# A hybrid decoder block on one core: first projection ahead of its norm, recurrence woven with attention, output projection in halves, first keys computed ahead of the ranking

## The chip, the cores and the metric

The kernel runs as one program on one core of a Trainium2 chip. The metric is the device time of that program in microseconds (us), as the median of the runs shown. TensorE is PE here (PEld is its weight loads), VectorE is DVE, ScalarE is ACT, GpSimd is POOL, SyncE is SP, whose queue issues nearly all transfers.

## The reference, cut to what matters

512 tokens of width 1024 go through one block:

```
h = rms_norm(x) ; p = h @ w_in                     # 2464 columns used, in 20 tiles of 128
rwkv columns: p + mu * (p[token - 1] - p), then a recurrence over tokens, 8 heads of 64
attention columns: + bias, window of 128 tokens, softmax with a sink, 8 query and 2 key heads
x = x + [y_rwkv, rms_norm(y_attn)] @ w_out
h2 = rms_norm(x)
per head (8), per half (2):  scores of 128 keys = (h2 @ wq) @ subkeys ; top 16 of each
best 16 of the 256 pairs -> softmax gates ; expert rows u, v ; y = sum gate * gelu(h2 . u) * v
out = rms_norm(x + y)
```

## The kernel before, in words

All float32 products of wide operands are made as three passes over operands split into a high part and a remainder (`split`, L163 to L166: a cast on ACT, then a subtraction on DVE or POOL; `mm3_`, L172 to L178: 8 chunks of 128 rows, three matmuls each, so 24 matmuls of 512 columns for one tile).

**Front.** `x` arrives transposed in eight pieces (L92). The first norm (`rms`, L208) sums squares over the chunks, takes the root on DVE (`rsqrt`) and broadcasts it over the partitions through PE; then each chunk of `x` is scaled by weight and root (L248) and split. `proj` makes one tile of columns; `shifted` (L286) mixes a tile with its previous token: two copies on ACT out of PSUM (L291, L293) and one combination on DVE (L294). `prepare(j)` makes the operands of head pair j, `products(j)` the triangular solves and products inside chunks of 64 tokens (L406 is the products `pg`, in tiles of 64 by 64 of the array). `weave` interleaves, in program order, the steps of `prepare(j+1)` and `products(j)`; for the last j, `attention_columns` stands for `prepare`. Then comes `recurrence()`, a chain over 8 chunks of 64 tokens (L614 to L646) with `group_norm` of each 128 tokens, and after it in program order `attention()`: 8 parts, each with scores (L676), mask (L678), maximum (L683), exponentials (L691), division by the sum on DVE (L698), transposes (L714), output (L720), and `out_norm` of each 128 tokens. Outside the blocks marked `manual_schedule`, a planner orders each engine's instructions when the kernel is built: what stands earlier in the program goes first among what it reckons ready, so later work fills gaps. PSUM tiles of the front come from four tags of two banks each (`proj`, `chain`, `tinv`, `att`); recurrence and `group_norm` use `chain` and `proj`.

**Turn to the retrieval.** The residual `x2T` is loaded (L815) when its SBUF, shared with the recurrence's tiles, comes free. The output projection makes 8 tiles of 512 tokens (L822 adds), each adding its square to the second norm's sum; then root, broadcast, 32 transposes of `x` to rows (L850), scaling by the norm (L858) and splits, three of eight remainders on DVE and five on POOL.

**Ranking.** A loop over 16 halves of heads (hc), in the order written out by hand on every engine: the key product `pq` (24 matmuls of 512), copy, scores `psc` (L1047), copy, and `top` on DVE (five kinds of instruction on four tiles, L929 to L937); between them `steps(ups, n)` puts in half products of the dense operand `pA` (12 matmuls of 384), and `choose` ranks pairs. Weights are loaded and split one to three hc ahead.

**Dense.** One-hots and gates are built on DVE while `pA` goes on; then 128 blocks of gated `v` are accumulated (L1269 to L1271). None of this is in the diff.

Of the kernel before, what the change touches and what calls it, by code (L numbers as in the profile page):

```python
# [13 lines left out]
OP = mybir.AluOpType  # L14
# [61 lines left out]
def _emit(ctx, tc, A, out, dbg, stop):  # L76
# [5 lines left out]
    keep = ctx.enter_context(tc.tile_pool(name="keep", bufs=1))  # L82
# [5 lines left out]

    xst, xp = right("xp")
# [6 lines left out]
    SY.dma_start(sink, A["sink"])  # L96
# [146 lines left out]
    rb = xp.tile([128, S], F32, name="rb")  # L243
    SC.copy(rb, pb)
    hhi, hlo = hl("h")
    for k in range(KD):
        h = xp.tile([128, S], F32, name="h", tag="h", bufs=3)
        V.scalar_tensor_tensor(h, xT[:, k, :], vcol(C_LN1 + k), rb, op0=OP.mult, op1=OP.mult)  # L248
        split(hhi[:, k, :], hlo[:, k, :], h)
    xst.close()  # L250
# [16 lines left out]
    def load_w(src, name="w"):  # L267
        his, los = [], []
        for hf in range(2):
            ks = slice(4 * hf, 4 * hf + 4)  # L270
            w = wst.tile([128, 4, 128], F32, name=name, tag="w", bufs=3)
            SY.dma_start(w, src[:, ks])
            whi = wst.tile([128, 4, 128], F32R, name=name + "h", tag="wh", bufs=4)
            wlo = wst.tile([128, 4, 128], F32R, name=name + "l", tag="wl", bufs=4)
            split(whi, wlo, w)
            his += [whi[:, k] for k in range(4)]
            los += [wlo[:, k] for k in range(4)]
        return his, los

    def proj(i, m=128):  # L280
        whi, wlo = load_w(A["w_in"][i])
        p = pt("proj", "pj")
        yield from mm3_(p[:m], whi, wlo, hhi, hlo, m=m)
        return p[:m]

    def shifted(i, dst, pool, m=128):  # L286

        p = yield from proj(i, m)
# [10 lines left out]
    pst, prep = right("prep")  # L299

# [8 lines left out]
    def lora():  # L309
        yield from shifted(0, la, prep)  # L310
# [81 lines left out]
    def products(j):  # L392
# [4 lines left out]
        for x in range(2):  # L397

            for ch in range(2):
                pg = pt("tinv", "pg", (128, 4, 128))  # L400
                for c in range(4):
                    ts = slice((4 * ch + c) * 64, (4 * ch + c) * 64 + 64)
# [4 lines left out]
                    if c == 1:  # L407
                        yield
                for p in range(2):
                    orow = slice(64 * p, 64 * p + 64)  # L410
                    for g_, cl in ((gA, slice(0, 64)), (gR, slice(64, 128))):
                        V.tensor_tensor(out=g_[orow, 4 * ch:4 * ch + 4, p ^ x, :], in0=pg[orow, :, cl],
                                        in1=gmask[orow, None, cl].to_broadcast([64, 4, 64]), op=OP.mult)
                yield
# [10 lines left out]
        BK = rwk.tile([128, 8, 2, 64], F32, name=f"BK{j}")  # L425
        for ch in range(2):
            pk = pt("tinv", "pk", (128, 4, 2, 64))
            for c in range(4):
                ts = slice((4 * ch + c) * 64, (4 * ch + c) * 64 + 64)
# [329 lines left out]
    for _ in recurrence():  # L759
        pass  # L760
# [638 lines left out]
```

## Time and profile before

| what | value |
|---|---|
| time, median of 3 runs | 1654.14 us (1652.88 to 1655.71) |
| the profiled execution's own time | 1651.63 us |
| its span | 1649.9 us |
| PE, PEld busy in the span | 96%, 83% |
| DVE, ACT, POOL busy | 78%, 40%, 43% |
| granted clock of PE, mean | 0.992 |

The shares are means over stages with different limits, and a matmul's modelled end reaches past the start of the next one, so a busy PE is not a full PE: its pace is read from starts. Times of rows count from the start of the span.

### The profile page before, as it was taken

To read this page: it belongs to the slowest core of one execution; us is meant where nothing else is said; L and a number is where in the kernel's file an instruction comes from. 1 tells how busy PE (TensorE), PEld (TensorE's weight loads), DVE (VectorE), ACT (ScalarE), POOL (GpSimd) and SP (SyncE) were. 2 spreads that over 40 slices of the span, in tenths; PEclk is the share of its full clock that TensorE was granted. 3 is DMA by queue.
4 is the path that set the end of the run, shared out by engine and by line. 5 is a ranking of instruction groups with operands and counts; after the bars stand their busy time and mean duration, and the time that the engine had idled before them with its cause. 6 is when DMAs were issued, how large, how long until landed. Compare 5 with 4: busy or idle time off the path is not lost.

```text
span 1649.9 us, 30181 instructions
## 1 busy us (share of the span) xinstructions
PE 1584.4 (96%) x11629; PEld 1362.9 (83%) x11629; DVE 1279.5 (78%) x2474; ACT 655.2 (40%) x1078; POOL 712.3 (43%) x670
## 2 busy tenths in 40 slices
PE   5999999898999989999999999999999999999997
PEld 4777677676898889888888888888888888888886
DVE  5656548745799989999868778877878877787797
ACT  5444345534343435445433333333333333333334
POOL 5112110033577612222235555555565655556582
PEclk9999999999999999999999999999999999999999
DMA  4111120141222249998999988988988989889794
GB/s 135 53 41 41 53 60 2 58 166 52 90 103 91 78 162 318 331 360 316 337 325 354 330 308 298 332 311 304 341 304 310 319 310 325 306 289 352 244 305 147
DMA packets 180113, 369.57 MB, mean 224 GB/s; under 512 B 17792, under 2 KB 102272, under 8 KB 179712
## 3 DMA queue, kind: packets, MB, share of 16 engines
q1 hardware_dynamic: 137056, 225.14, 40.0%
q0 software_dynamic: 36864, 134.23, 22.4%
q10 hardware_dynamic: 6048, 8.26, 1.4%
q8 instruction: 91, 1.49, 0.4%
q14 instruction: 54, 0.44, 0.1%
HBM read 332.04 MB, written 35.52 MB: 223 GB/s over the span
## 4 chain that ended last, share of the span: by engine, by line
PE 49%; DVE 11%; DMA 3%; issue 2%; ACT 1%; SPq 0%; POOL 0%; DVEq 0%; POOLq 0%; ACTq 0%
PE acc L1271 10%; PE acc L1269 10%; PE acc L1270 10%; PE pA L177 7%; PE pA L175 7%; PE pA L176 7%; DVE O L1140 3%; DVE ul L166 2%; DVE scr L1094 2%; DVE P L1145 2%; DMA u<-in_uT_dram 1%; DMA row<-in_vB_dram,ix 0%; DMA gts<-gates 0%; DMA acts<-actd 0%; PE pG L1167 0%
## 5 line engine op out<-in xcount | busy, mean ns | idle before, releaser
L177 PE MATMUL pA<-h2hi,ul 128*128 128x384 f32 x1024 | 348.3, 340 | 10.2 <-DVE ul L166 6.1
L175 PE MATMUL pA<-h2hi,uh 128*128 128x384 f32 x1024 | 354.0, 346 | 3.0 <-ACT uh L165 1.6
L176 PE MATMUL pA<-h2lo,uh 128*128 128x384 f32 x1024 | 346.4, 338 | 0.0
L1271 PE MATMUL acc<-vl,wh 128*128 128x512 f32 x768 | 299.1, 389 | 1.1 <-DVE vl L166 1.1
L1269 PE MATMUL acc<-vh,wh 128*128 128x512 f32 x768 | 299.5, 390 | 0.6 <-ACT vh L165 0.6
L1270 PE MATMUL acc<-vh,wl 128*128 128x512 f32 x768 | 299.3, 390 | 0.0
L1081 POOL DMA_INDIRECT row<-in_u_dram,ix x128 | 175.6, 1372 | 284.8 <-DVE scr L1094 246.5
L1081 POOL DMA_INDIRECT row<-in_vB_dram,ix x128 | 195.9, 1530 | 142.5 <-DVE x L1092 118.9
L166 DVE TENSOR_TENSOR vl<-v,vh 128x1024 fp32r<-128x1024 f32 x128 | 217.1, 1697 | 35.9 <-ACT vh L165 35.0
L177 PEld LDWEIGHTS pA<-h2hi,ul 128*128 128x128 f32 x1024 | 193.3, 189 | 15.3 <-DVE ul L166 11.2
L175 PEld LDWEIGHTS pA<-h2hi,uh 128*128 128x128 f32 x1024 | 193.4, 189 | 6.8 <-ACT uh L165 2.1
L176 PEld LDWEIGHTS pA<-h2lo,uh 128*128 128x128 f32 x1024 | 193.4, 189 | 3.0
L1092 DVE SCALAR_TENSOR_TENSOR x<-row,ac,x 128x1024 f32<-128x1024 f32 x128 | 172.6, 1348 | 6.0 <-DMA row<-in_vB_dram,ix 4.2
L1271 PEld LDWEIGHTS acc<-vl,wh 128*128 128x128 f32 x768 | 144.2, 188 | 32.6 <-DVE vl L166 2.1
L1269 PEld LDWEIGHTS acc<-vh,wh 128*128 128x128 f32 x768 | 144.2, 188 | 28.5 <-ACT vh L165 0.9
L1270 PEld LDWEIGHTS acc<-vh,wl 128*128 128x128 f32 x768 | 144.1, 188 | 27.4
L1094 DVE SCALAR_TENSOR_TENSOR scr<-row,h2g 128x1024 f32<-128x1024 f32 x128 | 158.8, 1240 | 1.5 <-DMA row<-in_u_dram,ix 0.2
L165 ACT CAST uh<-u 128x1024 fp32r<-128x1024 f32 x128 | 133.9, 1047 | 61.3 <-PE pA L176 33.0
L166 DVE TENSOR_TENSOR ul<-u,uh 128x1024 fp32r<-128x1024 f32 x109 | 134.8, 1238 | 21.2 <-ACT uh L165 20.9
L165 ACT CAST vh<-v 128x1024 fp32r<-128x1024 f32 x128 | 134.0, 1047 | 0.1
L1168 ACT ACTIVATE gst<-pG 128x512 f32<-128x512 f32 x96 | 55.9, 597 | 100.6 <-PE pG L1167 98.8
L888 ACT ACTIVATE act<-pA 128x384 f32<-128x384 f32 x86 | 42.2, 491 | 132.6 <-PE pA L177 132.6
(711 smaller groups left out, 2508.0 us busy)
## 6 DMA issues: line engine op xcount, KB each, us to landing
u<-in_uT_dram SPq DMA_DIRECT2D x128, 512.0 KB, 8.1
v<-in_vB_dram SPq DMA_DIRECT2D x128, 512.0 KB, 6.3
gts<-gates SPq DMA_DIRECT2D x384, 64.0 KB, 5.1
gates<-gst SPq DMA_DIRECT2D x11, 2048.0 KB, 11.8
w<-in_w_in_dram SPq DMA_DIRECT2D x40, 256.0 KB, 3.2
wq<-in_wq_dram SPq DMA_DIRECT2D x16, 512.0 KB, 3.5
acts<-actd ACTq DMA_DIRECT2D x42, 192.0 KB, 6.1
act<-acts SPq DMA_DIRECT2D x42, 192.0 KB
```

The lines of the kernel that those rows point to most:

```text
L165: (hi_eng or SC.copy)(dst_hi, src)
L166: (lo_eng or V).tensor_tensor(out=dst_lo, in0=src, in1=dst_hi.bitcast(F32), op=OP.subtract)
L175: mm(ps, whi[k][:, :m], ahi[:, k], start=k == 0, stop=False)
L176: mm(ps, whi[k][:, :m], alo[:, k], start=False, stop=False)
L177: mm(ps, wlo[k][:, :m], ahi[:, k], start=False, stop=k == KD - 1)
L1081: GP.indirect_dma_start(r_, None, A["vB"].rearrange("b p d -> (b p) d") if w_ else A["u"], bass.IndirectOffsetOnAxis(ap=ix[:, w_, jj:jj + ...
L1092: V.scalar_tensor_tensor(x2[:, 0, :], r_, ac[:, jj:jj + 1], x2[:, 0, :], op0=OP.mult, op1=OP.add)
L1094: V.scalar_tensor_tensor(scr, r_, 1.0, h2g, op0=OP.mult, op1=OP.mult, accum_out=ac[:, jj:jj + 1])
L1168: SC.activation(gst[:, :, :, t4 * 4:t4 * 4 + 4].rearrange("p n g t -> p (n g) t"), p.rearrange("p t e -> p e t"), AF.Copy, scale=1.0 / GS)
L1269: mm(o, wh[:, ts], vh[:, ds_], start=b == 0, stop=False)
L1270: mm(o, wl[:, ts], vh[:, ds_], start=False, stop=False)
L1271: mm(o, wh[:, ts], vl[:, ds_], start=False, stop=b == 127)
```

## The change

The first projection (column tile 0) is made from `x` times the norm's weight alone, ahead of the norm; the norm's factor `rb` is multiplied into every projected tile on DVE as it leaves PSUM, and ACT's copy goes. `products` issues its 64-by-64 products for both operands side by side. Attention keeps one key tile and takes 64 of its rows for each key head; its division moves to POOL. Recurrence and attention are woven. The output projection goes over tokens 0 to 255 first (tiles 5, 6, 7, 0 to 4), then over 256 to 511; the norm, transposes and key products of the first half stand among the second half's tiles, and key products 0 and 1 are done before the ranking. Key weights 2 and 3 and the first block of `u` are loaded and split earlier; `ln2r` is loaded later.

```diff
-    for k in range(KD):
-        SY.dma_start(xT[:, k, :], A["xT"][:, k, :])
     vec = consts.tile([128, NVEC], F32, name="vec")
     SY.dma_start(vec, A["vec"])
+    for k in range(2):
+        SY.dma_start(xT[:, k, :], A["xT"][:, k, :])
...
+    first[0] = load_w(A["w_in"][0])
+    for k in range(2, KD):
+        SY.dma_start(xT[:, k, :], A["xT"][:, k, :])
     take, scale, spread = rms(xp, KD, D, "n1", V)
-    for k in range(KD):
-        take(k, xT[:, k, :])
-    scale()
-    pb = spread()
...
-        V.scalar_tensor_tensor(h, xT[:, k, :], vcol(C_LN1 + k), rb, op0=OP.mult, op1=OP.mult)
+        V.tensor_scalar(h, xT[:, k, :], vcol(C_LN1 + k), None, op0=OP.mult)
         split(hhi[:, k, :], hlo[:, k, :], h)
+        take(k, xT[:, k, :])
+    with tc.manual_schedule(engines={mybir.EngineType.PE}):
+        p0 = proj(0)
...
+        scale()
+        pb = spread()
+    rb = prep.tile([128, S], F32, name="rb", tag="rb")
+    SC.copy(rb, pb)
...
-        SC.copy(pr[:m, 1:S + 1], p)
-        pm = pool.tile([128, S], F32, name="pm", tag="pm", bufs=1)
-        SC.activation(pm[:m], p, AF.Identity, scale=omu[:m, i:i + 1])
-        V.scalar_tensor_tensor(dst, pr[:m, 0:S], vec[:m, C_MU + i:C_MU + i + 1], pm[:m],
+        V.tensor_tensor(out=pr[:m, 1:S + 1], in0=p, in1=rb[:m], op=OP.mult)
+        SC.activation(dst, pr[:m, 1:S + 1], AF.Identity, scale=omu[:m, i:i + 1])
+        V.scalar_tensor_tensor(dst, pr[:m, 0:S], vec[:m, C_MU + i:C_MU + i + 1], dst,
...
+            pg = [pt("tinv", "pg", (128, 4, 128)) for x in range(2)]
+            for c in range(4):
+                for x in range(2):
                     for p in range(2):
-                        mm(pg[orow, c, :], (k if x else B)[rows, ts], AR[rows, 4 * ch + c, :], start=True, stop=True)
+                        mm(pg[x][orow, c, :], (k if x else B)[rows, ts], AR[rows, 4 * ch + c, :], start=True, stop=True)
...
-            SC.activation(q, p, AF.Identity, bias=vcol(C_BATT + j))
+            V.tensor_tensor(out=q, in0=p, in1=rb, op=OP.mult)
+            SC.activation(q, q, AF.Identity, bias=vcol(C_BATT + j))
...
-        weave(prepare(j + 1) if j < 3 else attention_columns(), WS[j], products(j), 23)
+        weave(prepare(j + 1) if j < 3 else attention_columns(), WS[j], products(j), 15)
...
-                mm(pS[kv][:, e, w0:], qT[2 * jj + e][:, tk], kP[kv][:, ks], start=True, stop=True)
+                rows = slice(64 * kv, 64 * kv + 64)
+                mm(pS[kv][:, e, w0:], qT[2 * jj + e][rows, tk], kP[rows, ks], start=True, stop=True)
...
-                V.tensor_scalar(Ps[:, kv, e, w0:], Ps[:, kv, e, w0:], sm[:, kv, e:e + 1], None, op0=OP.mult)
+                GP.tensor_scalar(Ps[:, kv, e, w0:], Ps[:, kv, e, w0:], sm[:, kv, e:e + 1], None, op0=OP.mult)
...
-    for _ in recurrence():
-        pass
-    for _ in attention():
-        pass
+    weave(recurrence(), 35, attention(), 64)
...
-            if hc < 2:
+            if hc < 4:
                 wqs[hc] = pool_u.tile([128, KD, 128], F32, name="wq", tag="u", bufs=4)
...
-    for i in range(KD):
-        whi, wlo = load_w(A["w_out"][i])
...
+    def out_weights(i):
+        if i < 2 or i > 4:
+            wo[i] = load_w(A["w_out"][i])
+            return
...
+    def out_tile(i, h):
+        whi, wlo = wo[i]
+        p = pt(("proj", "chain")[i % 2], "pj")[:, 0:256]
+        for _ in mm3_(p, whi, wlo, yhi[:, :, HS[h]], ylo[:, :, HS[h]]):
+            pass
+        V.tensor_tensor(out=xT[:, i, HS[h]], in0=xT[:, i, HS[h]], in1=p, op=OP.add)
+        square(i, h)
...
+    for i in (5, 6, 7, 0, 1, 2, 3, 4):
+        out_weights(i)
+        out_tile(i, 0)
     pe_ = ExitStack()
     pe_.enter_context(tc.manual_schedule(engines={mybir.EngineType.PE}))
+    out_tile(0, 1)
+    norm_sums(0)
+    wq_load(0)
+    wq_load(1)
+    out_tile(1, 1)
+    out_tile(2, 1)
+    pb = norm_spread(0)
...
+    for i in range(3, KD):
+        for k in range(2 * (i - 3), min(KD, 2 * (i - 2))):
+            rows(k, 0)
+            normed(k, 0, pb)
+        if i > 4:
+            out_weights(i)
+        out_tile(i, 1)
...
+    key_product(0, 0)
+    norm_sums(1)
+    key_product(1, 0)
+    pb = norm_spread(1)
     for k in range(KD):
+        normed(k, 1, pb)
+    for k in range(KD):
+        rows(k, 1)
+        if k == 3:
+            key_product(0, 1)
+    key_product(1, 1)
...
-        up_split(0)
         for n, b in enumerate(B):
...
-    wq_load(2)
+    up_split(0)
+    wq_split(2)
     for hc in range(16):
...
-        if hc:
+        if hc > 1:
             wq_split(hc + 1)
-        wq_load(hc + 3)
-        whi, wlo = wqs.pop(hc)
...
+        if hc:
+            wq_load(hc + 3)
+        if hc < 2:
+            q = q01[:, hc]
+        else:
+            whi, wlo = wqs.pop(hc)
...
+        if hc == 2:
+            ln2r = mp.tile([128, D], F32, name="ln2r", tag="lnr")
+            SY.dma_start(ln2r, A["ln2r"])
```

`normed(k, h)` scales and splits 256 tokens of chunk k, with the remainder on POOL where k is no multiple of 3; `rows(k, h)` makes two transposes; `norm_sums` and `norm_spread` are the norm's sum and broadcast for two tiles of 128 tokens; `square` adds squares, nearly all on POOL; `key_product(hc, h)` is `mm3_` over 256 columns with a copy into `q01`.

## Rows read from the trace of the kernel before

**Rows 1.** The busy time of each engine by stage: stretch, its length, then busy us (and instructions) of PE, PEld, DVE, ACT and POOL, the granted clock of PE, the transfers' share and GB/s.
```profile
51.00:237.00 186.00, 184.04 (x3587) 135.18 (x3586) 100.83 (x226) 74.75 (x138) 32.79 (x70) 1.00 0.16 49
237.00:296.00 59.00, 58.06 (x824) 43.94 (x823) 48.48 (x172) 32.86 (x106) 0.00 (x0) 1.00 0.04 11
296.00:335.00 39.00, 34.39 (x225) 25.25 (x225) 29.38 (x114) 20.19 (x53) 1.72 (x2) 0.96 0.19 68
335.00:371.00 36.00, 35.07 (x151) 27.93 (x149) 16.36 (x17) 11.75 (x19) 13.96 (x8) 1.00 0.51 183
391.00:428.00 37.00, 33.01 (x162) 27.29 (x163) 20.63 (x130) 12.22 (x17) 12.59 (x6) 1.00 0.28 100
428.00:546.00 118.00, 118.00 (x619) 105.89 (x618) 111.37 (x599) 45.38 (x62) 83.94 (x65) 1.00 0.26 90
840.00:1649.00 809.00, 799.31 (x3872) 706.92 (x3870) 644.13 (x646) 290.05 (x409) 462.12 (x339) 1.00 0.87 306
```

**Rows 2.** The timeline of the start: start, us, engine, line, operation, out<-in, shapes, count, and in brackets the idle time before it with what ended it.
```profile
3.68 0.63 ACT L215 ACTIVATE n1acc<-xT 128x512 f32<-128x512 f32 x1 [1.59 <-DMA xT<-in_xT_dram]
...
10.50 1.47 DVE L219 TENSOR_TENSOR n1acc<-n1acc,n1sq 128x512 f32<-128x512 f32 x2
...
20.06 0.59 ACT L244 COPY rb<-n1b 128x512 f32<-128x512 f32 x1 [1.85 <-PE n1b L231]
...
22.13 1.22 PE L175 MATMUL pj<-hhi,wh 128*128 128x512 f32 x2 [2.11 <-ACT hhi L165]
...
34.66 0.58 ACT L291 COPY pr<-pj 128x512 f32<-128x512 f32 x1
```

**Rows 3.** The groups of instructions of the first 410 us, shapes kept apart: busy us and mean ns of one, then the idle time before them.
```profile
L291 ACT COPY pr<-pj 128x512 f32<-128x512 f32 x13 | 7.6, 584 | 1.3 <-PE pj L177 0.7 <-DVE TT L479 0.5
L166 DVE TENSOR_TENSOR hlo<-h,hhi 128x512 fp32r<-128x512 f32 x8 | 5.1, 682 | 1.3 <-ACT hhi L165 1.3
L350 DVE TENSOR_TENSOR kk<-kk,pn 128x512 f32<-128x512 f32 x4 | 2.7, 687 | 5.2 <-PE pn L348 5.2
```

**Rows 4.** The timeline of PE alone, at two places of the front and one after the ranking; where a row has a count, its matmuls run up to the start of the next row.
```profile
43.38 1.05 PE L342 MATMUL kss<-hind,ksq 128*128 128x2 f32 x8
44.29 0.48 PE L176 MATMUL pj<-hlo,wh 128*128 128x512 f32 x1
...
60.82 1.96 PE L406 MATMUL pg<-AR,B 64*64 64x128 f32 x32
62.72 0.50 PE L175 MATMUL pj<-hhi,wh 128*128 128x512 f32 x1
...
572.02 0.34 PE L176 MATMUL pA<-h2lo,uh 128*128 128x384 f32 x1
572.20 0.34 PE L177 MATMUL pA<-h2hi,ul 128*128 128x384 f32 x1
```

**Rows 5.** The timeline from the recurrence's first step to the end of attention.
```profile
237.82 0.68 PE L614 MATMUL psa<-SAV,TF 64*64 64x64 f32 x16
...
295.45 0.37 ACT L638 COPY yT<-py 128x256 f32<-128x256 f32 x1 [0.67 <-PE py L636]
...
314.34 0.33 SPq L815 DMA_DIRECT2D x2T<-in_xT_dram  x1
...
316.29 0.68 DVE L166 TENSOR_TENSOR ylo<-yT,yhi 128x512 fp32r<-128x512 f32 x1
...
333.91 0.69 DVE L166 TENSOR_TENSOR ylo<-oT,yhi 128x512 fp32r<-128x512 f32 x1
```

**Rows 6.** The group of attention's division on DVE, in the 98 us from 237 to 335; the columns are those of rows 3.
```profile
L698 DVE TENSOR_SCALAR Ps<-Ps,st 128x256 f32<-128x256 f32 x24 | 7.9, 347 | 0.0
```

**Rows 7.** One instruction of DVE with POOL at work and with POOL idle, and POOL's instruction over it, from the timelines of these engines; then one of POOL's own groups by source line (ns: least, median, most).
```profile
472.06 2.41 POOL L166 TENSOR_TENSOR ul<-u,uh 128x1024 fp32r<-128x1024 f32 x1
473.28 1.27 DVE L993 TENSOR_TENSOR sg__4943<-sg__4943,fi 128x64 f32<-128x64 f32 x1
...
599.27 0.22 DVE L993 TENSOR_TENSOR sg__4943<-sg__4943,fi 128x64 f32<-128x64 f32 x1
...
L460 POOL TENSOR_TENSOR Lb<-LC,lmask x16: 725/740/978, 65.8 to 217.6; 128x256 f32<-128x256 f32 x16
```

**Rows 8.** The timeline from the last output tile to the first scores of the ranking.
```profile
364.51 0.69 DVE L822 TENSOR_TENSOR x2T<-x2T,pj 128x512 f32<-128x512 f32 x1 [4.31 <-PE pj L177]
...
370.11 0.69 DVE L822 TENSOR_TENSOR x2T<-x2T,pj 128x512 f32<-128x512 f32 x1 [4.91 <-PE pj L177]
...
375.86 2.07 PE L231 MATMUL n2b<-ident,n2rs 128*128 128x128 f32 x8 [0.54 <-DVE n2rs L205]
377.72 4.50 PE L850 MATMUL px<-ident,x2T 128*128 128x128 f32 x20
...
382.65 7.17 POOL L166 TENSOR_TENSOR h2lo<-h,h2hi 128x512 fp32r<-128x512 f32 x5 [15.28 <-ACT h2hi L165]
...
391.28 1.16 PE L1047 MATMUL psc<-subk,q 128*128 128x128 f32 x8 [0.68 <-ACT q L1042]
```

**Rows 9.** The timeline of the ranking's second and fifth pass: scores on PE, and the start of `top` on DVE.
```profile
402.76 1.05 PE L1047 MATMUL psc<-subk,q 128*128 128x128 f32 x8
...
428.45 1.05 PE L1047 MATMUL psc<-subk,q 128*128 128x128 f32 x8
430.20 0.87 DVE L929 MAX8 tv<-sc 128x8 f32<-128x128 f32 x4 [5.60 <-ACT sc L1049]
```

More of the change, by code (lines that the diff above doesn't have):

```diff
@@ L519, in attention_columns @@
     def attention_columns():
[L520 to L522 removed]
+        kP = late["kP"] = prep.tile([128, S], F32, name="kP", tag="aup")
         gup = late["gup"] = prep.tile([128, S], F32, name="gup", tag="la")
@@ L832, in _emit @@
-    take(KD - 1, xT[:, KD - 1, :])
-    if stop == "x2":
-        for j in range(KD):
-            SY.dma_start(dbg["y"][:, j, :], yhi[:, j, :].bitcast(F32))
-        SY.dma_start(dbg["x2"], xT)
-        x2st.close()
-        pust.close()
-        mpst.close()
-        front.close()
-        return
+    acc2 = x2p.tile([128, S], F32, name="n2acc")
+    rs2 = consts.tile([128, NT], F32, name="n2rs")
+    wo = {}
+    HS = [slice(0, 256), slice(256, 512)]
+    TS = [(0, 1), (2, 3)]
+    hhi2, hlo2 = None, None
@@ new lines, in out_weights, with square @@
+    def out_weights(i):
+        if i < 2 or i > 4:
+            wo[i] = load_w(A["w_out"][i])
+            return
+        w = x2p.tile([128, KD, 128], F32, name="wo", tag="wo", bufs=2)
+        SY.dma_start(w, A["w_out"][i])
+        whi = x2p.tile([128, KD, 128], F32R, name="woh", tag="woh", bufs=3)
+        wlo = x2p.tile([128, KD, 128], F32R, name="wol", tag="wol", bufs=3)
+        split(whi, wlo, w)
+        wo[i] = [whi[:, k] for k in range(KD)], [wlo[:, k] for k in range(KD)]
+    def square(i, h):
+        cs = HS[h]
+        if i == (5, 0)[h]:
+            SC.activation(acc2[:, cs], xT[:, i, cs], AF.Square)
+            return
+        sq = x2p.tile([128, 256], F32, name="n2sq", tag="n2sq", bufs=2)
+        SC.activation(sq, xT[:, i, cs], AF.Square)
+        (V if i == (4, 7)[h] else GP).tensor_tensor(out=acc2[:, cs], in0=acc2[:, cs], in1=sq, op=OP.add)
@@ new lines, in norm_spread, with rows, normed @@
+    def norm_spread(h):
+        p = pt("att", "n2b", (128, 256))
+        for j, t in enumerate(TS[h]):
+            mm(p[:, j * 128:(j + 1) * 128], rs2[:, t:t + 1].to_broadcast([128, 128]), ident, start=True, stop=True)
+        return p
+    def rows(k, h):
+        p = pt("tinv", "px2", (128, 2, 128))
+        for j, t in enumerate(TS[h]):
+            PE.transpose(p[:, j, :], xT[:, k, t * 128:(t + 1) * 128], ident)
+        SC.copy(x2[:, 2 * h:2 * h + 2, k * 128:(k + 1) * 128], p)
+    def normed(k, h, pb):
+        x = x2p.tile([128, 256], F32, name="h2", tag="h2", bufs=4)
+        V.scalar_tensor_tensor(x, xT[:, k, HS[h]], vcol(C_LN2 + k), pb, op0=OP.mult, op1=OP.mult)
+        split(hhi2[:, k, HS[h]], hlo2[:, k, HS[h]], x, lo_eng=GP if k % 3 else V)
@@ new lines, in key_product @@
+    def key_product(hc, h):
+        whi, wlo = wqs[hc]
+        p = pt(("proj", "chain")[hc], "pq")[:, 0:256]
+        for _ in mm3_(p, [whi[:, k] for k in range(KD)], [wlo[:, k] for k in range(KD)],
+                      hhi2[:, :, HS[h]], hlo2[:, :, HS[h]]):
+            pass
+        SC.copy(q01[:, hc, HS[h]], p)
+    for i in (5, 6, 7, 0, 1, 2, 3, 4):
+        out_weights(i)
+        out_tile(i, 0)
+    hhi2 = h2p.tile([128, KD, S], F32R, name="h2hi")
+    hlo2 = h2p.tile([128, KD, S], F32R, name="h2lo")
@@ L860, in _emit @@
+    norm_sums(1)
+    key_product(1, 0)
+    pb = norm_spread(1)
+    for k in range(KD):
+        normed(k, 1, pb)
[4 more added lines that the diff above has]
+    key_product(1, 1)
+    for hc in range(2):
+        wqs.pop(hc)
+    hhi, hlo = hhi2, hlo2
+    pe_.close()
     front.close()
+    kst.close()
     x2st.close()
@@ L1329, in _emit @@
     pust.close()
+    h2st.close()
     mpst.close()
```

153 lines of the change are left out of this document (71 added, 82 removed).

## The prediction

> **What bounds the kernel now.** I read the busy time by stage first, to see which engine fills which stretch. Up to 237 us PE is nearly full (184.04 of 186 us, modelled) with DVE at half; from 237 to 335 us DVE carries most (48.48 + 29.38 = 77.9 of 98 us), PE has gaps and POOL does 1.7 us; from 335 to 371 PE is full with the output projection; between 391 and 428 DVE works only 20.63 of 37 us; from 428 to 546 PE is full with DVE at 111.37 of 118; behind 840 PE is full to the end [rows 1]. So a time saved ahead of the ranking moves everything behind it forward, and nothing behind it shrinks. Then I read the timeline at the four joints where the front waits: the start, where PE's first projection waits for the norm until 22.13 us [rows 2]; the end of recurrence and attention, where the recurrence's last output is copied at 295.45, its norm ends at 316.97 and attention alone runs on to 334.60 [rows 5]; the second norm, 21.2 us from the last output tile (370.11) to the first scores (391.28) [rows 8]; the first passes of the ranking [rows 9].
>
> **Start (1 us gained, -2 to +4).** Before, the chain is norm, then scaling, then projection. After, PE can start when the first chunk and weights are split, at some 7 us (first chunk landed at 3.68, one small and two weight transfers squeeze in). But DVE now does scaling, remainder and square-add per chunk before PE ends: 8 x 3 x 0.68 = 16.4 us, with two weight remainders of the same size 17.8, so the sum is ready at about 22.5. The norm's own chain, from the last square-add (10.50 + 1.47 = 11.97) to `rb` (20.65), is 8.7 us [rows 2]: `rb` at 31. The first tile left PSUM at 34.66 before; now at 31.5, but the second projection stands behind the norm's matmuls on PE and starts about when it did. One us.
>
> **Products and projections (4 us, -3 to +8).** 19 more evacuations multiply by `rb` on DVE, 0.687 each [rows 3]: 13 us on an engine half free; ACT sheds 13 x 0.584 = 7.6. PE issued 32 of the 64-by-64 products in 1.90 us, 0.059 each [rows 4]; 256 of them are 15.2 us. Side by side in four quarters of the array they take half at best, 7.6 less, and nothing less at worst. The solves' steps are a chain that this doesn't shorten; I take half. The low end is the 13 us of DVE landing partly on waits. Fewer steps in the weave (15 for 23) cost nothing while the count matches the yields.
>
> **Recurrence and attention (12 us, -5 to +20).** The division leaves DVE: 24 x 0.347 = 8.3 us, and eight of half the width, at most 2.8 [rows 6]: 10. DVE's work falls from 77.9 to 68 us. At the share it reached from 237 to 296 (48.48 of 59, 82%) [rows 1] that takes 83 us, and the stage would end at 237.8 + 83 = 321 where it ended at 334.6: 14. The weave gives this by spreading attention so that it has no tail alone behind the recurrence. The score matmuls on 64 rows save PE some time, which is not the bound there: nothing.
> POOL takes 32 divisions. The trace shows none on POOL; between DVE's 0.347 [rows 6] and POOL's two-input product of the same size, 0.740 [rows 7], I take 0.55: 18 us of POOL, which is free, but each part's transposes come 0.8 us later, two parts ahead of need. There is a price: the same DVE addition took 0.22 us with POOL idle and 1.27 with POOL at work [rows 7]. POOL is at work 18 of 83 us, and DVE's two-input instructions meet it for some 2 us in sum: 12 stay. The Trainium skill ("SBUF — State Buffer", on the shared port pair) makes this an exclusive lock: the one that comes second waits for the whole instruction of the other, which the pair of rows agrees with; by it POOL's 18 us could be taken off DVE in the worst case, which is the third case below.
>
> **Output projection to first scores (4 us lost; from 31 lost to 7 gained).** A tile cost 5.60 us (370.11 - 364.51) [rows 8], 0.233 per matmul of 512; one of 384 costs 0.176 [rows 4]; so one of 256 by the same step 0.119. Weights of 128 columns with 2 moving columns came every 0.114 (8 in 0.91 us) [rows 4], so loading them just allows that; the other bound is 0.176, at which the halves would cost 27 us more. At 0.119 a half tile costs 2.86 and halving costs nothing.
> The first half could run beside attention, but its sums need `x2T`, whose transfer was issued at 314.34 when the recurrence's norm released its place [rows 5], and its PSUM tags are the recurrence's. I let two half tiles (5.7 us) be done when the stage ends and 39.1 of the 44.8 us be left, where before 35.5 were left (334.60 to 370.11). Added in between: 16 transposes at 4.50 / 20 = 0.22, 3.6 us, and 1 us of the first half's sums and broadcast. Behind the last half tile: key 0 and key 1 on the first half, 5.7 us, which cover the root; 1.5 of waiting and broadcast; eight chunks scaled and split at POOL's pace, 5 x 7.17 / 10 = 3.6, with the key product ending some 5 us on; transposes 1.8; the last half product 2.9: 17. In sum 60.7 us to the first scores where 56.7 were (334.60 to 391.28): 4 lost. Three weight tiles are loaded and split twice; 1.5 MB and 3 x 2 x 0.68 us of DVE lie under a PE-bound stretch with DVE at 16.36 of 36 [rows 1]; if that cover fails it is 4 us. On SP's queue key weights 2 and 3 wait for slots that keys 0 and 1 free, and the repeated weights stand behind them; that wait ends with a split that needs no output tile.
>
> **First passes of the ranking (8.4 us gained, 5 to 10).** From scores 0 to scores 1 took 402.76 - 391.28 = 11.5 us: the second key product and a wait for the dense operand's split. Now only scores (1.0) and a dense half product, 12 x 0.176 = 2.1, stand there: 3.1. Passes 1 to 4 keep their 25.7 us (to 428.45). DVE follows: it has 16 us idle in that stretch [rows 1], 5.60 of them ahead of the fifth pass [rows 9]. From there on PE's order is the old one. `ln2r` on SP waits only for scores 1: nothing.
>
> **Sum.** 1 + 4 + 12 - 4 + 8.4 = 21.4 us. The profiled execution took 1651.63 us (span 1649.9 and 1.7 around it), 2.5 below the median 1654.14; so 1630.2 by its own time and 1632.7 by the median. I say 1632.
>
> **Rivals.** *The first half is free.* If `x2T` lands before attention ends, six more half tiles (17 us) run in PE's gaps; the gaps would hold some 11. For it: the recurrence is the longer chain's owner of that place and may end early. Against: the weave ends both together. Time 1632 - 11 = 1621.
> *The weave is there already.* Attention filled the recurrence's gaps before, and DVE at 82% may be what the planner gives; with POOL's 18 us taken back from DVE by waits, the stage ends where it did. Time 1632 + 12 = 1644. For it: DVE's rows with POOL at work.
> *Weights bound the halves.* If 256 columns don't come under 0.176, the 20 half products (480 matmuls) cost 480 x 0.057 = 27 us more: 1659, slower. It decides from 0.119 + 21.4 / 480 = 0.164 on. Against: 0.114 for weights alone.
> *Weaving slows the recurrence.* Eight chunks took 57.6 us, 7.2 each; each of three steps may now stand behind an attention instruction on DVE. The other terms give 9.4, so the kernel is slower once the stage ends later than 344; at 12 us a chunk it ends with the norm's 21.5 at 355, 20 late: 1654 - 9.4 + 20 = 1665. Against: the chain's instructions are first whenever they are ready at their turn.
> *Nothing moves*: the stage stays, and the products take DVE's load: within 0.2% of 1654.
>
> **Chances.** The forecast 0.50, the first half free 0.16, the weave there already 0.20, weights 0.04, recurrence slowed 0.05, nothing 0.05. A measurement of this kernel can tell about 0.2% (3.3 us) from no change. Faster is the first three, 0.86; same 0.05; slower 0.09. The range reaches from the second case with its products' high end, 1608, to the third with the products' low end, 1651.
>
> **What would show it.** The first projection's start near 7 us but the first tile out of PSUM near 31; `pg` at 0.03 to 0.06 per matmul; the last remainder of attention near 321, close to the recurrence's norm; matmuls of 256 columns every 0.12 us; `x2T` issued at the end of the recurrence's norm; about 61 us from attention's end to scores 0; scores 1 about 3 us behind scores 0; from the fifth pass on the old pace of PE. Wrong would be: an end of attention past 334, half matmuls above 0.16, or scores 0 to 4 still 37 us apart.

## The result and the profile after

The changed kernel takes 1631.15 us (median of four runs, 1630.73 to 1631.52), the kernel before 1653.51 beside it: a ratio of 0.9865, 95% interval 0.9849 to 0.9882, or 22.4 us. A second set of runs took 1632.52, ratio 0.9875 [0.9859, 0.989]. The forecast was 1632, in a range from 1608 to 1651, so it is 1 us off. The sum is better than its terms, as the stages show: that it comes so near is in part luck. The profiled execution took 1630.73 us, its span 1629.0.

The busy time by stage of the changed kernel, in the columns of [rows 1], cut at its own joints:
```profile
51.00:226.00 175.00, 172.73 (x3561) 128.63 (x3561) 106.54 (x235) 65.64 (x121) 29.87 (x65) 1.00 0.16 50
226.00:293.00 67.00, 64.48 (x863) 47.98 (x861) 53.96 (x173) 38.67 (x130) 26.15 (x31) 1.00 0.02 7
293.00:319.00 26.00, 25.99 (x235) 23.18 (x235) 20.90 (x85) 14.96 (x32) 2.67 (x4) 1.00 0.30 101
319.00:363.00 44.00, 39.08 (x318) 38.91 (x319) 24.29 (x49) 19.29 (x42) 19.74 (x19) 0.96 0.41 151
363.00:380.00 17.00, 15.26 (x114) 13.41 (x113) 8.22 (x26) 8.46 (x22) 5.43 (x36) 1.00 0.35 116
380.00:409.00 29.00, 27.65 (x149) 23.98 (x149) 19.31 (x129) 10.64 (x15) 12.50 (x6) 1.00 0.32 114
409.00:526.00 117.00, 117.00 (x624) 105.95 (x623) 111.90 (x600) 44.65 (x61) 84.52 (x65) 1.00 0.26 91
```
Recurrence and attention (226 to 319) hold 53.96 + 20.90 = 74.9 us of DVE, where [rows 1] have 77.9 before; POOL now does 28.8 us there. From 409 on each engine's load is as before.

The timeline of the start, the answer to [rows 2]:
```profile
9.15 0.79 PE L176 MATMUL pj<-hhi,wh 128*128 128x512 f32 x1 [9.15 <-ACT hhi L166]
...
21.54 0.95 PE L225 MATMUL n1ss<-ones,n1acc 128*128 128x1 f32 x8
...
22.34 0.48 PE L178 MATMUL pj<-hhi,wl 128*128 128x512 f32 x1
...
25.69 1.05 PE L232 MATMUL n1b<-ident,n1rs 128*128 128x128 f32 x8
26.78 0.59 ACT L283 COPY rb<-n1b 128x512 f32<-128x512 f32 x1 [0.79 <-PE n1b L232]
27.40 0.69 DVE L307 TENSOR_TENSOR pr<-pj,rb 128x512 f32<-128x512 f32 x1 [0.69 <-ACT rb L283]
```
The first tile leaves PSUM at 27.40 (34.66 before), and the row at 22.34 belongs to the second projection, which runs while DVE works out the root.

The timeline of recurrence, attention and the first output sums, the answer to [rows 5]:
```profile
225.85 0.68 PE L626 MATMUL psa<-SAV,TF 64*64 64x64 f32 x16
...
292.08 0.37 ACT L650 COPY yT<-py 128x256 f32<-128x256 f32 x1 [0.89 <-PE py L648]
...
313.59 0.33 SPq L826 DMA_DIRECT2D x2T<-in_xT_dram  x1
...
316.80 0.68 DVE L167 TENSOR_TENSOR ylo<-yT,yhi 128x512 fp32r<-128x512 f32 x1
317.49 0.69 DVE L167 TENSOR_TENSOR ylo<-oT,yhi 128x512 fp32r<-128x512 f32 x1
...
322.23 1.41 DVE L860 TENSOR_TENSOR x2T<-x2T,pj 128x256 f32<-128x256 f32 x4 [3.45 <-DMA x2T<-in_xT_dram]
...
322.80 0.55 PE L176 MATMUL pj<-yhi,wh 128*128 128x256 f32 x1 [3.81 <-DVE x2T L860]
```
Both chains now end together (0.69 us apart), and the new wait stands in the last two rows: `x2T`, issued at 313.59 when the recurrence's norm frees its place, is there 8.6 us later, at 322.23, and PE stands still for 3.81.

TensorE alone, at the first scores of the ranking's passes 0, 1 and 4, the answer to [rows 8, 9]:
```profile
380.42 1.06 PE L1132 MATMUL psc<-subk,q 128*128 128x128 f32 x8
383.42 0.83 PE L1132 MATMUL psc<-subk,q 128*128 128x128 f32 x6
...
408.66 1.05 PE L1132 MATMUL psc<-subk,q 128*128 128x128 f32 x8
```

From such rows of every profiled run come the marks below, in us, rounded to 0.1 before they are subtracted: the way from the first `pg` to the first `psa`, from there to the end of the last `ylo` (the stage's end), from there to scores 0, the two together, and scores 0 to scores 4; then the first `pg`, scores 0, and the median of the timed runs. Scores 0 count from their first weight load, at most 0.13 ahead of the matmul's row.
```
                       pg-psa  psa-ylo  ylo-sc0  psa-sc0  sc0-sc4  first pg  sc0     median
before                 177.0    96.8     56.7    153.5     37.0     60.8    391.3   1653.5
changed                172.2    92.4     62.1    154.5     28.2     53.6    380.3   1631.2
changed, again         172.2    92.4     63.0    155.4     28.2     53.1    380.7   1632.5
weave undone           172.6   100.6     55.1    155.7     28.1     54.0    382.3   1633.8
division on DVE        172.2   100.6     62.7    163.3     28.2     52.9    388.4   1638.9
both undone            172.5   110.7     49.9    160.6     28.1     53.8    386.9   1637.9
norm first             174.4    94.2     61.1    155.3     28.2     62.1    391.8   1645.1
products as before     178.9    92.4     60.5    152.9     28.2     53.4    385.2   1640.0
keys 0, 1 late         172.2    92.4     64.1    156.5     35.2     52.8    381.5   1641.4
x2T in 8, SP           172.6    93.9     62.7    156.6     28.2     53.9    383.1   1632.3
x2T in 8, GpSimd       172.5    92.1     57.6    149.7     28.2     53.2    375.4   1629.5
  and weave undone     172.5   108.0     50.7    158.7     28.2     53.4    384.6   1636.8
  and weave 35 to 48   172.2   110.9     50.6    161.5     28.2     53.5    387.2   1635.5
before + weave + div.  177.5    91.5     67.7    159.2     37.1     61.3    398.0   1657.9
```
Where nothing was touched, the way from `pg` to `psa` repeats within 0.4 us and scores 0 to scores 4 within 0.1, but the first `pg` itself only within 1.2, and the way from `psa` to scores 0 differs by 0.9 between the two profiles of the changed kernel. Behind the ranking, from `pG` (the first products of the dense stage) to the end, these two differ by 3 us (1047.3 and 1050.3), so for a single part the marks say more than the total. Each row of marks is one execution; those of "weave undone", "x2T in 8, SP", "weave 35 to 48" and the last row are 3 to 5 us longer than the median of their kernel.

### The profile page after: what moved, and what is told of

The parts are those of the page before. It is cut to its first block, busy times and chain, and to the rows that moved or that the text cites. A ratio compares the mean times of both kernels' runs of the same rounds, so it can differ in the third digit from the quotient of the medians.

```text
span 1629.0 us, 30768 instructions
## 1 busy us (share of the span) xinstructions
PE 1572.6 (97%) x11869; PEld 1366.7 (84%) x11869; DVE 1286.1 (79%) x2497; ACT 652.5 (40%) x1092; POOL 742.4 (46%) x711
## 4 chain that ended last, share of the span: by engine, by line
PE 50%; DVE 11%; DMA 3%; issue 1%; ACT 1%; POOL 1%; SPq 0%; DVEq 0%; ACTq 0%
PE acc L1359 10%; PE acc L1358 10%; PE acc L1357 10%; PE pA L178 7%; PE pA L176 7%; PE pA L177 7%; DVE O L1228 3%; DVE ul L167 2%; DVE scr L1182 2%; DVE P L1233 2%; DMA u<-in_uT_dram 2%; DMA row<-in_vB_dram,ix 1%; DMA v<-in_vB_dram 0%; PE pG L1255 0%; POOL row L1169 0%
## 5 line engine op out<-in xcount | busy, mean ns | idle before, releaser
L176 PE MATMUL pA<-h2hi,uh 128*128 128x384 f32 x1024 | 350.3, 342 | 1.5 <-ACT actd L969 1.5
L1169 POOL DMA_INDIRECT row<-in_u_dram,ix x128 | 175.2, 1369 | 285.7 <-DVE scr L1182 247.7
L167 DVE TENSOR_TENSOR vl<-v,vh 128x1024 fp32r<-128x1024 f32 x128 | 213.9, 1672 | 35.2 <-ACT vh L166 34.4
L178 PEld LDWEIGHTS pA<-h2hi,ul 128*128 128x128 f32 x1024 | 192.8, 188 | 14.8 <-DVE ul L167 10.5
## 6 DMA issues: line engine op xcount, KB each, us to landing
gates<-gst SPq DMA_DIRECT2D x11, 2048.0 KB, 11.5
```

The costliest lines, as they stand in the source:

```text
L167: (lo_eng or V).tensor_tensor(out=dst_lo, in0=src, in1=dst_hi.bitcast(F32), op=OP.subtract)
L176: mm(ps, whi[k][:, :m], ahi[:, k], start=k == 0, stop=False)
L178: mm(ps, wlo[k][:, :m], ahi[:, k], start=False, stop=k == KD - 1)
L1169: GP.indirect_dma_start(r_, None, A["vB"].rearrange("b p d -> (b p) d") if w_ else A["u"], bass.IndirectOffsetOnAxis(ap=ix[:, w_, jj:jj + ...
```

## Experiments

**The weave alone undone, and the division alone put back.**
```
-    weave(recurrence(), 35, attention(), 64)
+    for _ in recurrence(): pass
+    for _ in attention(): pass
```


> The changed kernel with the weave alone undone: recurrence first, then attention, as in the kernel before; the division stays on GpSimd. Theory A, the written weave is what shortens this stage: the recurrence goes back to some 7.2 us a chunk (8.3 in the changed kernel), attention again ends alone some 17 us behind the recurrence's norm, the stage from the first psa to the last ylo goes from 92.4 back to 96.8 us or, with DVE's division gone, to 94, and the time to 1633 to 1636. Rival B, the scheduler mixes the two anyway and the weave does nothing: stage 92.4, time 1630 to 1632. Rival C, the weave harms, since it slows the recurrence's chain by 1.1 us a chunk: time under 1629.

Measured: 1633.84 us (1629.26 to 1637.83), ratio 0.9869 [0.985, 0.9887]. The stage is 8.2 us longer, as A said and more, but scores 0 come only 2.0 later: the norm of the recurrence ends at 312.8, `x2T` comes earlier, and half tiles run beside attention's tail. So the stage's end is a poor mark for this part. In the total the intervals of this kernel and the changed one overlap, and the way from `psa` to scores 0 (155.7) is hardly longer than in the changed kernel's two profiles (154.5 and 155.4) although the clock is at its lower level from 240.9 to 247.7 in this execution. A gain of the weave alone is not shown here.
```
-                GP.tensor_scalar(Ps[:, kv, e, w0:], Ps[:, kv, e, w0:], sm[:, kv, e:e + 1], ...)
+                V.tensor_scalar(Ps[:, kv, e, w0:], Ps[:, kv, e, w0:], sm[:, kv, e:e + 1], ...)
```


> The changed kernel with attention's 32 divisions back on VectorE (0.347 us each before; 0.925 median on GpSimd). Theory A, DVE sets this stage and the division's move is its gain: DVE gets back 24 x 0.347 and 8 x 0.2, 10 us in all, and at its share of 80% the stage is 8 to 12 us longer: 1639 to 1643. Rival B, the division on GpSimd costs as much by its length (32 x 0.925 in the parts' chain, and DVE's two-input work waiting beside it) as it takes off DVE: stage within 1.5 us, 1630 to 1632.5. Rival C, it costs more than it takes off: under 1629.

Measured: 1638.85 us (1633.53 to 1644.33), ratio 0.9909 [0.9886, 0.9932]; the stage is 8.2 us longer and scores 0 are 8.1 later: theory A in the stage, just short of its range in the total. The busy time of this run's recurrence, in the columns of [rows 1], shows a second loss:
```profile
225.00:240.00 15.00, 13.89 (x187) 9.82 (x186) 13.93 (x43) 9.27 (x38) 0.00 (x0) 1.00 0.11 31
240.00:252.50 12.50, 12.33 (x111) 8.24 (x111) 6.55 (x18) 3.53 (x10) 0.00 (x0) 0.63 0.00 1
252.50:263.00 10.50, 10.50 (x107) 7.57 (x106) 6.78 (x27) 3.88 (x14) 0.00 (x0) 0.63 0.01 2
```
At 1.00 both engines are nearly full (DVE 13.93 of 15, PE 13.89). From 240 the granted clock is at its lower level (1.2 GHz) for most of 23 us, 0.63 in the mean, and there PE is full and DVE busy for 13.3 of 23. The chunk from 240.0 to 252.5 takes 12.5 us against 7.9 in the changed kernel. How much of the 8.2 is DVE's work and how much the clock, this run cannot part.

**Both undone**, which leaves that stage as before but for the score products on 64 rows.


> The changed kernel with both the weave and the division on GpSimd undone, so that this stage is as before but for the score products on 64 rows. The two undone one at a time each took the stage from 92.4 to 100.6 us, where the kernel before took 96.8. Theory A, each needs the other, and what costs is the granted clock falling inside the recurrence, not the instructions: with both undone the stage is 95 to 98 us again at full clock, scores 0 come at 378 to 382 as x2T is issued at the end of the recurrence's norm ahead of attention's tail, time 1631 to 1636. Rival B, the two add up and some other part of the change costs 12 us here: stage 107 to 110, time 1643 to 1649.

Measured: 1637.88 us, ratio 0.9911 [0.9896, 0.9925]. The stage of 110.7 falls beyond B's range, but scores 0 at 386.9 and the time fit neither: A's mark was 382 at the latest, B's time 1643 at the least. Attention's tail ends late while half tiles run beside it (145 of the output projection's 384 matmuls come before the stage's end, 91 in the changed kernel), which gives `ylo` to scores 0 in 49.9 us; that the half tiles push it out is argued, not shown. By the way from `psa` to scores 0, moving the division is worth 8.8 us under the weave (163.3 - 154.5) and 4.9 without it (160.6 - 155.7), the clock's falls included; the weave is worth 1.2 us with the division on GpSimd, close to the 0.9 by which that way repeats, and costs 2.7 with it on DVE.

**The two parts alone, on the kernel before** (the two edits above, the other way round).


> The kernel before with two parts of the change alone: recurrence and attention woven, and attention's division on GpSimd. In the changed kernel, undoing both made the way from the first psa to the first scores 6.1 us longer (160.6 against 154.5). Theory A, the two parts give those 6 us here too: 147 to 149 us from the first psa to the first scores where the kernel before has 153.5, time 1645 to 1649. Rival B, they give nothing without the halves: recurrence and attention now end together, x2T is issued when the norm ends and lands 8 us later, and nothing is left that covers it: the first output sum waits 3 to 5 us with the clock falling, 152 to 155 us, time 1650 to 1654.

Measured: 1657.88 us, ratio 1.002 [1.0007, 1.0034]: slower by 0.2%. Rival B is right that the two give nothing by themselves, and more was lost than it said, but not by the wait that it named. The stage is 5.3 us shorter (91.5), the way from its end to scores 0 is 11.0 longer. The busy time of its stretches around the stage's end:
```profile
239.00:318.00 79.00, 74.57 (x958) 57.27 (x954) 63.24 (x218) 46.58 (x148) 28.54 (x34) 1.00 0.02 7
318.00:331.00 13.00, 9.40 (x47) 7.94 (x48) 7.97 (x33) 3.85 (x9) 0.00 (x0) 0.50 0.20 58
331.00:339.00 8.00, 8.00 (x28) 6.31 (x27) 1.37 (x3) 1.24 (x2) 0.00 (x0) 0.74 0.99 410
```
`x2T` is issued at 327.52 where it was issued at 314.34 [rows 5], the transfers are full behind it (0.99), and the first output sum runs at 338.93, 8.7 us behind the stage's end; before it ran 3.1 behind (337.7). But from its first matmul of the output projection, at 328.99, PE shows no stop, so the transfer cost it no wait. What is lost is the work that attention's tail had held. TensorE's busy time in the output projection's matmuls (tile `pj`) up to the stage's end, then the granted clock and the transfers, in the kernel before and in this one:
```profile
290.00:334.61 44.61, 12.61 (x41) 0.96 0.17 60
290.00:330.27 40.27, 1.28 (x3) 0.85 0.05 13
```
Of 192 matmuls 41 were issued by then, now 3: 38 at 0.233 are 8.9 us. PE has 47 matmuls in the 13 us from 318 and a clock of 0.50; the clock stays low until 335, and the first matmuls of the output projection come 0.427 apart (329.58 to 334.70), an estimated 2.4 us more. Together these are 11.3, about the 11.0.

**`x2T` in eight loads.** First on SP's queue:
```
+    for i in (5, 6, 7, 0, 1, 2, 3, 4): xTs[i] = x2p.tile([128, S], F32, ...)
-    SY.dma_start(xT, A["xT"])
+    for i in (5, 6, 7, 0, 1, 2, 3, 4): SY.dma_start(xTs[i], A["xT"][:, i, :])
```


> The changed kernel with x2T as eight tiles and eight loads, in the order in which the output tiles are made (5, 6, 7, 0 to 4), in place of one load of 2 MB that waits for the last reader of any part of its place. Theory A, most of that place is free when the recurrence ends, some 25 us earlier: the stall of TensorE at 318.8 to 322.8 and the half clock up to 325.5 behind it go, scores 0 come at 374 to 377 instead of 380.3, time 1625 to 1628. Rival B, the first piece lies over what the last norm reads and the others stand behind it on the same queue: scores 0 at 380 and 1630 to 1632. Rival C, the half tiles that can now run sooner take TensorE and VectorE from the recurrence's and attention's last steps, and the stage ends later by what is gained: 1629 to 1632 with the last ylo past 320.

Measured: 1632.34 us, ratio 0.9867 [0.985, 0.9883]; scores 0 at 383.1. B in its effect, but not by the piece it named. The timeline of SP's queue:
```profile
301.23 13.30 SPq L243 DMA_DIRECT2D w<-in_w_out_dram  x4
314.58 3.99 SPq L829 DMA_DIRECT2D x2T<-in_xT_dram  x8
```
All eight stand behind four weight loads, whose waits for DVE's splits reach to 314.58; that six of the pieces were free before shows in the next run. So the same loads were put on GpSimd's queue (`GP.dma_start`).


> The changed kernel with x2T as eight loads again, but issued on GpSimd's queue instead of SP's. With eight loads on SP's queue nothing was gained: they stood behind the output projection's weight loads, whose own waits end at 314.6, and the first was issued at 314.58. GpSimd has done its last division some 40 us before that. Theory A, the place of most pieces is free when the recurrence's last chunk is done (292): the first pieces land before 310, TensorE's stall at 318.8 to 322.8 and the half clock behind it go, and scores 0 come 4 to 6 us earlier, at 374.5 to 377 where the changed kernel had 380.3 and 380.7: 1626 to 1629. Rival B, the pieces are early but the stage's end is not waiting for them: the half tiles take TensorE's and VectorE's time from the last norm and attention, and scores 0 come at 379 to 381: 1630 to 1633. Rival C, one of the pieces waits for the last norm and GpSimd's queue stands still behind it, so that the square-adds of the second norm come late: later than 382, over 1634.

Measured: 1629.50 us (1626.50 to 1631.59), ratio 0.9851 [0.9835, 0.9867]; scores 0 at 375.4, 4.9 earlier: theory A by its mark, 0.5 us past its range in the time. (GpSimd's last division had ended 18 us before the loads on SP's queue, not 40.) The timeline of GpSimd, and the busy time of the stretch behind the stage's end:
```profile
290.22 3.68 POOL L711 TENSOR_SCALAR Ps<-Ps,st 128x256 f32<-128x256 f32 x4 [1.19 <-DVE rsq L202]
293.85 2.96 POOL L829 DMA_DIRECT2D x2T<-in_xT_dram  x5
...
313.41 1.07 POOL L829 DMA_DIRECT2D x2T<-in_xT_dram  x2 [14.35 <-DVE vro L206]
```
```profile
318.00:358.00 40.00, 38.48 (x321) 37.87 (x321) 21.56 (x50) 18.28 (x42) 18.95 (x19) 1.00 0.38 134
```
Six of the eight go 15 to 20 us earlier, PE's stop is gone, and the clock stays at 1.00 (0.96 in the changed kernel from 319 to 363). No half tile comes earlier: TensorE's matmuls of the output projection up to the stage's end (columns as in the two rows of `pj` above), in the changed kernel and in this one, are the same 91 of 384:
```profile
290.00:318.18 28.18, 13.36 (x91) 1.00 0.25 81
290.00:317.78 27.78, 13.36 (x91) 1.00 0.43 139
```
So the 4.9 us are the stop (3.8) and the slow matmuls behind it (1.1). This is the fastest version run, 24.3 us under the kernel before beside it. Against the changed kernel the intervals overlap, so there only the mark is sure.

**Two other orders on top of it.**
```
-    weave(recurrence(), 35, attention(), 64)
+    for _ in recurrence(): pass              # first kernel
+    for _ in attention(): pass
+    weave(recurrence(), 35, attention(), 48) # second kernel
```


> The changed kernel with x2T's eight loads on GpSimd's queue (1629.5; scores 0 at 375.4) and the weave undone. Without the weave the recurrence's norm ends some 5 us earlier (312.8 against 317.5) and attention's tail runs alone; with one late load of x2T that cost 2 us at scores 0 (382.3 against 380.3), and TensorE's clock fell inside the recurrence. Theory A, with x2T early the half tiles of the first half fill attention's tail and the weave is not needed: scores 0 at 372 to 376, 1626 to 1630. Rival B, attention's tail sets the end of the second half's input whatever fills it, and the clock falls in the recurrence as before: scores 0 at 377 to 381, 1631 to 1635.

> The changed kernel with x2T's eight loads on GpSimd's queue and the weave at 35 to 48 steps in place of 35 to 64: the recurrence is placed a third faster against attention, so that its norm ends before attention does. Theory A, the end of this stage is set by the recurrence's chain and its norm, and half tiles can fill a short tail of attention: the recurrence's last chunk at 284 to 289 instead of 291.4, scores 0 at 371 to 375, 1625 to 1629. Rival B, the order of the steps matters only where both are ready, and the stage is set by the work of TensorE and VectorE together: scores 0 within 1 us of 375.4, 1628 to 1631. Rival C, an attention tail leaves TensorE thin and its clock falls: scores 0 past 377.

Measured: 1636.77, ratio 0.9896 [0.9881, 0.9911], scores 0 at 384.6; and 1635.51, ratio 0.9897 [0.9882, 0.9913], scores 0 at 387.2. Rival B, later than it said, and rival C. Both leave attention a tail (the stage is 108.0 and 110.9 long), and both lose the clock inside the recurrence. Without the weave and with 35 to 48, in this order:
```profile
240.00:252.00 12.00, 12.00 (x114) 7.87 (x114) 6.12 (x26) 4.76 (x19) 2.43 (x5) 0.72 0.01 1
```
```profile
282.00:300.00 18.00, 18.00 (x139) 14.22 (x133) 9.41 (x38) 7.08 (x25) 3.66 (x4) 0.62 0.04 8
```
So the even weave is worth 9.0 us from `psa` to scores 0 (158.7 - 149.7) once `x2T` is early (7.3 between the medians), the clock's falls included, where 1.2 was all that showed with the late load.

**The first norm ahead of the first projection again.**
```
-        V.tensor_scalar(h, xT[:, k, :], vcol(C_LN1 + k), None, op0=OP.mult)
+        V.scalar_tensor_tensor(h, xT[:, k, :], vcol(C_LN1 + k), rb, op0=OP.mult, op1=OP.mult)
...
-        V.tensor_tensor(out=pr[:m, 1:S + 1], in0=p, in1=rb[:m], op=OP.mult)
+        SC.copy(pr[:m, 1:S + 1], p)
```


> The changed kernel with the first norm ahead of the first projection again: h is scaled by rb before it is split, and no projection is multiplied by rb behind its product (19 products of 0.69 us less on DVE). The early load of the first weights and the order of the loads stay. Theory A, the deferred norm alone gave the start's 7.2 us: first pg again at about 60 us, of which DVE's relief gives back 0 to 2 behind it: 1636 to 1638. Rival B, the order of the loads gave most of it: 1631 to 1633. Rival C, the deferred norm also gave the 4.8 us between the first pg and the first psa, since ACT shed 13 evacuations: 1641 to 1644.

Measured: 1645.06 us, ratio 0.9954 [0.9937, 0.9972]. First `pg` at 62.1 (8.5 later), first `psa` at 236.5 (10.7 later), scores 0 11.5 later. Nearest to C: the deferred norm gives the start's gain, and 2.2 us behind it although it adds 13 us to DVE. In this execution the clock is at its lower level from 159.1 to 162.5, which can make up to an estimated 1.7 us of the 2.2 (half of 3.4). Its ACT evacuations were not taken away by themselves either, so what gives the 2.2 is not shown.

**The products' loops as before.**
```
-            pg = [pt("tinv", "pg", (128, 4, 128)) for x in range(2)]
+        for x in range(2):
+            for ch in range(2):
+                pg = pt("tinv", "pg", (128, 4, 128))
...
-        weave(..., WS[j], products(j), 15)
+        weave(..., WS[j], products(j), 23)
```


> The changed kernel with the products' loops as before: B's products over both halves of the sequence, then k's (one PSUM tile at a time), pk one half after the other, 23 steps in the weave. Theory A, putting B's and k's products side by side gave the 4.8 us between the first pg and the first psa: the first psa comes at 230 to 231 instead of 225.8, and the time is 1635 to 1637. Rival B, PE's order at run time splits most of them apart again (in the changed kernel only the first chunk of the first head pair ran its groups of four in 0.11 us) and the 4.8 us came from elsewhere: first psa within 1 us of 225.8, time 1630.5 to 1632.5.

Measured: 1640.02 us, ratio 0.9919 [0.9902, 0.9936]; first `psa` at 232.3, 6.5 later, scores 0 4.9 later. Theory A, somewhat larger; up to an estimated 1.7 us of it can be the clock, which is at its lower level from 138.0 to 141.4 in this execution. The edit puts back three things at once, the loops of `pg`, those of `pk` and the steps of the weave, and does not part them.

**Keys 0 and 1 back in the ranking.**
```
-    key_product(0, 0)
     norm_sums(1)
-    key_product(1, 0)
...
-            q = q01[:, hc]
+            mm3(p, ..., hhi, hlo)
```


> The changed kernel with the products of keys 0 and 1 back in the ranking, whole, behind the second norm; their weights are still split ahead. Theory A, the forecast's two terms: the output projection to scores 0 falls from 62.2 by the 11.4 us of the four half products, of which some 5 covered the root and come back as waiting, plus one whole key product (5.7) ahead of scores 0: 61 to 63; scores 0 to scores 4 go from 28.3 back to 33 to 36: time 1636 to 1640. Rival B, the work is only moved: VectorE's ranking starts as much sooner as it then waits, 1630 to 1633. Rival C, TensorE idles through the second norm and its clock falls there as it did in the kernel before (0.59 from 374 to 380): 1640 to 1645.

Measured: 1641.41 us, ratio 0.9926 [0.9912, 0.994]. Scores 0 to scores 4 take 7.0 us more (35.2), yet scores 0 come 1.2 later, although 11.4 us of half products left their way and 5.7 came back. Rival C: the busy time from the last output tile to the first scores of this kernel:
```profile
361.00:381.00 20.00, 13.78 (x48) 9.66 (x48) 8.42 (x26) 7.41 (x20) 4.42 (x36) 0.74 0.23 79
```
PE has 48 matmuls in 20 us and its clock falls, as it does in the kernel before between 371 and 391 (15.99 us busy, 0.83). With the half products there it holds 1.00 (363 to 380 above). The early keys fill a gap that would otherwise be spent waiting and then at the lower clock.

## Why the forecast was right, step by step

**Start: 1 forecast, 7.2 measured** (first `pg` 60.82 to 53.60). The step that failed is that the second projection stands behind the norm's matmuls and starts about when it did. It ran in the root's gap, ahead of `n1b`, in spite of the order written out for PE. PE began later than forecast (9.15, not 7), but the sum ended earlier, at 20.31, not 22.5, of which eight scalings at 0.480 where 0.68 was taken are 1.6, and the chain from there to `rb` was 7.1 us, not 8.7. Part of that is PE: the same eight matmuls of the norm took twice as long in the kernel before, whose PE had done nothing ahead of them. From its timeline:
```profile
12.11 1.84 PE L224 MATMUL n1ss<-ones,n1acc 128*128 128x1 f32 x8 [12.11 <-DVE n1acc L219]
...
17.97 2.05 PE L231 MATMUL n1b<-ident,n1rs 128*128 128x128 f32 x8 [4.02 <-POOL lmask L143]
```
They take 0.95 and 1.05 in the changed kernel. The clock column reads 1.00 in both, so here it is the durations that speak.

**Products and projections: 4 forecast, 4.8 measured** (177.0 to 172.2). Right in size, and the edit of the products carries it: 6.7 us are lost without it. The pace gives only a part: counted from each start to PE's next, the 256 products hold PE for 14.8 us, and 17.0 before, 2.2 less where 3.8 was taken. What gives the rest is not shown. Half of their time was the guess. TensorE alone, at the first pair's products, shows both cases:
```profile
53.60 0.33 PE L419 MATMUL pg<-AR,B 64*64 64x128 f32 x2
53.62 0.33 PE L419 MATMUL pg<-AR,k 64*64 64x128 f32 x2
...
54.43 0.28 PE L419 MATMUL pg<-AR,k 64*64 64x128 f32 x2
...
56.46 1.09 PE L419 MATMUL pg<-AR,B 64*64 64x128 f32 x16
58.37 1.09 PE L419 MATMUL pg<-AR,k 64*64 64x128 f32 x16
```
The first 32 go in (54.43 - 53.60) / 30 = 0.028 us each, half of the 0.059 of [rows 4]; the next 32 were split into B's and k's again by the order in which PE's work was placed, and take the old pace. The parts do not add up: the way is 2.6 us shorter than before with the norm first (177.0 to 174.4), and 6.7 longer without the products' order when the norm is deferred; in both of these executions the clock falls once.

**Recurrence and attention: 12 forecast, 4.4 measured.** The share of DVE was right (from the first `psa` to the last `ylo` it is busy 74.3 of 92.4 us, 80%, for 82% taken); the work was mis-sized, 68 us for 74.3. The division's 32 records add up to 10.6 us, but they lie partly over their neighbours: without them the time in which DVE is busy on that way falls from 77.9 to 71.4 only. And 2.9 us of other work moved in, two more weight remainders and one evacuation among it. 74.3 / 0.82 = 90.6 us would have been the stage. On GpSimd one division takes 0.925, not 0.55 (the group by source line; ns: least, median, most):
```profile
L711 POOL TENSOR_SCALAR Ps<-Ps,st x32: 598/925/1302, 234.4 to 293.1; 128x256 f32<-128x256 f32 x24, 128x128 f32<-128x128 f32 x8
```
The 2 us set down for DVE meeting GpSimd came to 1.6: the sum, over DVE's instructions beside a division, of what they took above the median of their kind. It falls on the small ones: up to 0.41 us for the root's 0.16. A two-input one with a PSUM operand took the same as before (its group, columns as above):
```profile
L620 DVE TENSOR_TENSOR X<-SAV,px x14: 405/420/426, 230.8 to 288.6; 64x256 f32<-64x256 f32 x14
```
The Trainium skill ("SBUF — State Buffer", "SBUF: two separate sides") has the later of the two block until the other is done, for the instructions that take the shared pair. The small instructions agree with it in kind. The worst case that the forecast set beside it, GpSimd's whole time taken off DVE, is not what this kernel shows: 1.6 us of 27.7.

**Output projection to scores 0: 4 lost forecast, 5.4 measured** (56.7 to 62.1). The pace held: 12 half matmuls from 327.04 to 328.46, 0.118 each for 0.119 forecast, so the rival that weights bound the halves fell. Not two half tiles (48 matmuls) but 91 matmuls were done by the stage's end, 5.1 us better. Not in the sum was what comes next: the wait for `x2T`, 3.8 us, and 12 matmuls at 0.213 behind it, 1.1 us; the eight loads on GpSimd's queue give back 4.9. Another 1.6 us is not accounted for (60.7 - 5.1 + 4.9 = 60.5 for 62.1).

**First passes: 8.4 forecast, 8.8 measured** (37.0 to 28.2); scores 1 come 3.0 behind scores 0, for 3.1. **Behind them 0 forecast**, 1.3 measured up to the sixteenth pass and 1.1 to the first `pG`; the dense stage's 1.3 the other way lies within the 3 us by which it differs between two runs.

So the start came out 6 us above its term and the stage 8 below, and the total hides both. Of the rivals, the first half made free is worth 4.9 us and not 11, by a stop that goes and not by more half tiles ahead of the stage's end, and the change as it stands doesn't reach it. That the weave is there already is not refuted for the written weave: undone by itself it costs little more than the marks repeat by, and put on the kernel before with the division alone it makes that kernel slower; only with `x2T` early is it worth 9.0. The recurrence did slow, from 7.8 to 9.0 us a chunk (237.8 to 292.4 and 225.8 to 288.7 over seven), far from the 12 of that rival. The low end of the range does not come out of its own words: 1621 less the 4 us by which the products' high end passes their term is 1617, not 1608. The measured time lies inside either way.

## What to carry to other kernels

Two chains that are made to end together also release everything at once: look which transfer waits for that end, which queue it stands in, and what work the tail that goes had held, before counting the gain. Work moved into a gap of TensorE can cost nothing, where the gap would be followed by matmuls at the lower clock. Busy time to be taken off an engine is the time its records cover alone, not the sum of their durations.

## What the runs showed that was not expected

TensorE's granted clock falls inside the recurrence in some orders: 23 us at 0.63 with the division on DVE, 18 at 0.62 with the weave at 35 to 48, 12 at 0.72 without the weave; in both profiled runs of the changed kernel it stays at 1.00 there. Runs of those kernels spread by 3 to 11 us, those of the changed kernel by 0.8 and 3.2. Of the changed kernel's second set a spread within 2 us had been expected. What sets the fall off is not settled: in the first case PE is shown as busy ahead of it (13.89 of the 15 us up to 240).
